# Moving operands of the weight matmuls in two, four or eight parts, at other addresses modulo 256

## The chip, the cores and the metric

One core of a Trainium2 chip runs the kernel. The time is device time in microseconds of one execution, as the median of several; lower is better. The kernel before takes 845.64 us, the median of 3 runs (844.99 to 845.87).

## What is computed

Two transformer blocks over 256 tokens of width 1024, in float32. What matters here is that nearly all the work is products of the activations with weight matrices, 139 MB of which are read once.

```python
def first_block(x, ...):
    h = rms_norm(x, norm_mix_pre[l])
    proj = h @ w_in[l]                       # attention, recurrence and gate columns
    ...
    merged = (gates[..., :D] * (o_sb @ w_sb_out[l]) + gates[..., D:] * (o_rw @ w_rw_out[l]))
    x = x + rms_norm(merged @ w_o[l], norm_mix_post[l])
    h = rms_norm(x, norm_ffn_pre[l])
    f = (jax.nn.silu(h @ w_ffn_gate[l]) * (h @ w_ffn_up[l])) @ w_ffn_down[l]
    x = x + rms_norm(f, norm_ffn_post[l])

def second_block(x, mem, ...):
    x = x + hybrid_mixer(rms_norm_2(x, g_mix), w_in, conv_w, g_attn_out, g_conv_out, w_out)
    x = x + memory_cross_attention(rms_norm_2(x, g_xattn), rms_norm_2(mem, g_mem), w_q_mem, w_kv_mem, w_o_mem)
    x = x + squared_relu_mlp(rms_norm_2(x, g_mlp), w_up, w_down)
    return rms_norm_2(x, g_final)
```

## The kernel before, in words

Activations lie feature by token: a tile `[128, chunks, 256]` holds 128 features of each chunk on the partitions and its 256 tokens along the row. Weights come in slabs of 128 x 1024 float32 (512 KB): `slab` (line 182) loads one into `wraw` from the SyncE queue (L192), ScalarE rounds it to float32r in `whi` (L193), VectorE takes the remainder into `wlo` (L194). Activations are split in the same way into a hi and a lo tile by `split` (L277, L278), or by `scaled` with a gain (L325, L326). A product is then three matmuls for each 128 rows: `whi` with hi, `whi` with lo, `wlo` with hi. `block` (line 240) issues them (L258): the weight block of 128 x 128 is the stationary operand, the activation chunk of 256 tokens the moving one, so a slab of 256 columns and 512 rows is 24 matmuls. With `tok` the sides are exchanged: the activations are stationary, 128 tokens at a time, and the weights move (256 columns). The last matrix, `w_down_2`, is done that way too with 512 moving columns (`tokens`, through `mm`, L273); `ah` and `al` are the stationary side there.

The tiles in question: `xh`, `xl` hold the normed input of most products; `gh`, `gl` that of the first recurrence columns; `zh`, `zl` half of the merged branches; `sh`, `sl`, `oh`, `ol` the two branch outputs; `memh`, `meml` the memory; `fh`, `fl` the gated hidden rows of the first block (22 chunks); `yh`, `yl` the mixer's and `xoh`, `xol` (names in the trace of `oh`, `ol` in `cross`) the cross attention's output; `ah`, `al` the hidden rows of the last block (32 chunks).

The order of the work is the order of the code: `plan` lists the slabs, `next_slab` keeps three ahead, and smaller steps of the recurrence and the attentions are woven in between slabs. Each engine runs its instructions in program order.

Addresses are set by the order of allocation and by `shift` (line 119), which allocates a spare tile of a given number of bytes. Before the change the weights `whi` and `wlo` begin at multiples of 256 bytes, all tiles named above except `ah` and `al` at 192 past one, and `ah`, `al` at 64 past one. A chunk's row is 1024 bytes, so each chunk of a tile begins at the same place modulo 256.

Of the kernel before, what the change touches and what calls it, by code (L numbers as in the profile page):

```python
# [17 lines left out]
P = 128  # L18
T = 256
# [71 lines left out]


class Net:
    def __init__(self, ctx, tc, io):
        self.tc, self.nc, self.io = tc, tc.nc, io
        self.last_table = None
        self.queue, self.ready = [], []
        self.t2 = 3
        self.side = None
        nc = self.nc  # L100
        pool = lambda name, bufs=1, **k: ctx.enter_context(tc.tile_pool(name=name, bufs=bufs, **k))
        self.keep = pool("keep")
        self.cst = self.keep.tile([P, NRES], F32, name="cst")
        self.vec = self.keep.tile([P, NVEC], F32, name="vec")
        self.small = self.keep.tile([P, 8], F32, name="small")
        self.ones = self.keep.tile([P, P], F32, name="ones")
        self.pr = pool("wraw", 3)
        self.ph = pool("whi", 4)
        self.pl = pool("wlo", 4)


        acts = pool("acts")
        self.shift(acts, PHASE)
        self.xh = acts.tile([P, KC, T], F32R, name="xh")
        self.xl = acts.tile([P, KC, T], F32R, name="xl")
        self.zh = acts.tile([P, NP, T], F32R, name="zh")
        self.zl = acts.tile([P, NP, T], F32R, name="zl")

# [123 lines left out]
    def block(self, ps, name, g, b, xh, xl, tok):  # L242
        per = blocks(name)
        hi, lo, k0, m = self.next_slab(name, g * per + b)
        if isinstance(xh, list):
            xh, xl = xh[b], xl[b]
        cols = width(name) // P
        for c in range(cols):
            cc = slice(c * P, (c + 1) * P)
            for k in range(m):  # L250
                for t, (w, a) in enumerate(((hi, xh), (hi, xl), (lo, xh))):
                    first = b == 0 and c == 0 and k == 0 and t == 0
                    last = b == per - 1 and c == cols - 1 and k == m - 1 and t == 2
                    if tok:
                        lhsT, rhs = a[:, k0 + k, cc], w[:, k, :]
                    else:
                        lhsT, rhs = w[:, k, cc], a[:, k0 + k, :]
                    self.nc.tensor.matmul(ps[:, c, :], lhsT, rhs, start=first, stop=last,  # L258
                                          skip_group_check=True)

# [14 lines left out]
    def split(self, src, hi, lo):  # L275

        self.nc.scalar.copy(hi, src)  # L277
        self.nc.vector.tensor_sub(lo, src, hi.bitcast(F32))  # L278
# [13 lines left out]

    def rstd_sum(self, pool, parts, width, tag, square=None):

        ps = self.ax("ssum")
        for i, p in enumerate(parts):
            self.mm(ps[:, :T], self.ones, p, start=i == 0)
        lg = pool.tile([P, T], F32, tag="t1", name="lg", bufs=1)
        r = pool.tile([P, T], F32, tag=tag, name=tag)
        self.act(lg, ps[:, :T], AF.Ln, bias=self.eps, scale=1.0 / width)  # L300
        self.act(r, lg, AF.Exp, scale=-0.5)
        if square is not None:
            self.act(square, lg, AF.Exp, scale=-1.0)
        return r
# [15 lines left out]
    def scaled(self, src, gname, hi, lo, first=0):  # L320

        for i, s in enumerate(src, first):
            for j in range(2):
                k, g = 2 * i + j, self.v(gname, 2 * i + j)
                self.nc.scalar.activation(hi[:, k, :], s[:, j, :], AF.Copy, scale=g)  # L325
                self.nc.vector.scalar_tensor_tensor(lo[:, k, :], s[:, j, :], g, hi[:, k, :].bitcast(F32),  # L326
                                                    op0=ALU.mult, op1=ALU.subtract)
# [16 lines left out]
    def normed(self, pool, src, r, gname, hi, lo):  # L344

        for i, s in enumerate(src):
            h = pool.tile([P, 2, T], F32, tag="t2", name="nh", bufs=self.t2)
            for j in range(2):
                self.nc.vector.scalar_tensor_tensor(
                    h[:, j, :], s[:, j, :], self.v(gname, 2 * i + j), r, op0=ALU.mult, op1=ALU.mult)  # L350
            self.split(h, hi[:, 2 * i:2 * i + 2, :], lo[:, 2 * i:2 * i + 2, :])

# [74 lines left out]
def first(n):  # L427
    nc, tc = n.nc, n.tc
    with ExitStack() as ctx:
# [4 lines left out]
        one = ctx.enter_context(tc.tile_pool(name="one", bufs=1))  # L434
        n.shift(one, 608)
        s4 = ctx.enter_context(tc.tile_pool(name="s4", bufs=14))
        dr = ctx.enter_context(tc.tile_pool(name="dr", bufs=1, space=DRAM))
        n.shift(ctx.enter_context(tc.tile_pool(name="gap", bufs=1)), 640)

# [14 lines left out]
        xg = start.enter_context(tc.tile_pool(name="xg", bufs=1))  # L454
        gh = xg.tile([P, KC, T], F32R, name="gh")
        gl = xg.tile([P, KC, T], F32R, name="gl")
        n.scaled(xp, "norm_mix_pre", gh, gl)
# [317 lines left out]
        nc.scalar.copy(idb, n.c("ident"))  # L775
        sh = b4.tile([P, NP, T], F32R, tag="b4", name="sh")
        sl = b4.tile([P, NP, T], F32R, tag="b4", name="sl")
        pz, zm = {}, {}
# [27 lines left out]
        def sb_values(j):  # L806
            wt = zm[j][1]
            po = n.sx("po")
            for t, o, wc in ((0, slice(0, T), slice(0, T)), (1, slice(P, T), slice(T, 384))):
                for r_, rr in enumerate(half):  # L810
                    i = 2 * j + r_
                    n.mm(po[rr, o], vs_[:, t, 64 * i:64 * i + 64], wt[:, r_, wc], start=t == 0)
            of = tmp.tile([P, T], F32, tag="c2", name="of", bufs=3)
            nc.vector.tensor_copy(of, po[:, :T])
            n.split(of, sh[:, j, :], sl[:, j, :])

# [153 lines left out]
        def normalized():  # L970
# [3 lines left out]
            nc.sync.dma_start(flat(gb), park[1])  # L974
            oh, ol = norm["o"] = [s4.tile([P, NP, T], F32R, tag="s4", name=k) for k in ("oh", "ol")]
            pv = {}
# [11 lines left out]
            for i in range(2):  # L988
# [9 lines left out]
                nc.vector.tensor_add(yi, yi, gb[:, ii, :])  # L998
                n.split(yi, oh[:, ii, :], ol[:, ii, :])
            yield  # L1000
# [13 lines left out]
        for g in range(4):  # L1014
# [5 lines left out]
            hi, lo = (n.zh, n.zl) if g < 2 else (n.xh, n.xl)  # L1020
            n.split(t, hi[:, 2 * g:2 * g + 2, :], lo[:, 2 * g:2 * g + 2, :])

# [29 lines left out]
def ffn(n, tmp, wide, filler):  # L1052
    nc, tc = n.nc, n.tc
    with tc.tile_pool(name="ffn", bufs=1, reuse_waits="tile") as pool:
# [4 lines left out]
        n.table("silu_and_others")  # L1059
        fh = pool.tile([P, FF // P, T], F32R, name="fh")  # L1060
        fl = pool.tile([P, FF // P, T], F32R, name="fl")
        for g in range(FF // 256):
# [7 lines left out]
            nc.vector.tensor_mul(m, m, s)  # L1070
            n.split(m, fh[:, 2 * g:2 * g + 2, :], fl[:, 2 * g:2 * g + 2, :])
        n.table("natural_log_exp_and_others")
# [3 lines left out]
def memory(n, mem, wide, tmp, kT, vm):  # L1076
# [3 lines left out]
    nc.scalar.dma_start(m.rearrange("p c t -> p (c t)"), n.io["mem"])  # L1080
    mh = mem.tile([P, KC, T], F32R, name="memh")
    ml = mem.tile([P, KC, T], F32R, name="meml")
    n.scaled(pairs(m), "g_mem_2", mh, ml)
    acc = n.squares(tmp, pairs(m))
    r = pair(n.rstd_sum(mem, [acc], D, "rk"))
    rt = n.rstd_tok(mem, [acc], D, out=n.small[:, 4:6])
# [17 lines left out]
def hybrid(n, tmp, kv):  # L1104
    nc, tc = n.nc, n.tc
    with ExitStack() as ctx:
        pool = ctx.enter_context(tc.tile_pool(name="hyb", bufs=1, reuse_waits="tile"))
        yh = pool.tile([P, KC, T], F32R, name="yh")
        yl = pool.tile([P, KC, T], F32R, name="yl")
        r2 = pool.tile([P, T], F32, name="r2")  # L1110
        rs = []

        def norms():
            acc = n.squares(tmp, pairs(n.x))
            rs.append(pair(n.rstd_sum(pool, [acc], D, "rm", r2)))
            rs.append(n.rstd_tok(pool, [acc], D))
# [89 lines left out]
        def conv_norm():  # L1206
            rc = n.rstd(tmp, pairs(cv), 512, "rs")
            kv(4, n.ax("kv").rearrange("p (c t) -> p c t", c=2))
            n.normed(tmp, pairs(cv), rc, "g_conv_out_2", yh[:, NP:, :], yl[:, NP:, :])

# [3 lines left out]
def cross(n, tmp, kT, vm, kv):  # L1214
    nc, tc = n.nc, n.tc
    with ExitStack() as ctx:
        pool = ctx.enter_context(tc.tile_pool(name="xat", bufs=1, reuse_waits="tile"))
        oh = pool.tile([P, KC, T], F32R, name="xoh")
        ol = pool.tile([P, KC, T], F32R, name="xol")
        n.scaled(pairs(n.x), "g_xattn_2", n.xh, n.xl)  # L1220
# [52 lines left out]
        def values(h):  # L1273
# [8 lines left out]
            hh = slice(2 * h, 2 * h + 2)  # L1282
            nc.scalar.copy(oh[:, hh, :], po)
            nc.vector.tensor_sub(ol[:, hh, :], po, oh[:, hh, :].bitcast(F32))

# [15 lines left out]
def mlp(n, tmp, out):  # L1301
    nc, tc = n.nc, n.tc
    with ExitStack() as ctx:
        pool = ctx.enter_context(tc.tile_pool(name="mlp", bufs=1, reuse_waits="tile"))
        n.shift(pool, 832 - PHASE)
        ah = pool.tile([P, 32, T], F32R, name="ah")
# [144 lines left out]
```

## Time and profile before

| what | value |
|---|---|
| median of 3 runs | 845.64 us |
| the profiled execution's own time | 845.12 us |
| its span | 843.4 us |
| TensorE busy | 97% of the span, 6508 matmul records |
| weight loads busy | 92% |
| VectorE, ScalarE busy | 67%, 55% |
| DMA | 142.88 MB, mean 169 GB/s |

The span runs from the first to the last instruction of the profiled execution; 1.7 us of its time lie outside. Busy time counts an instruction from start to end. Matmuls are pipelined: one starts long before the one ahead of it ends, so the mean duration of a matmul (some 280 ns) is not its price. The distance from one start to the next is, and the chain in order of time shows it as the time of a piece divided by its count. A matmul of float32 operands leaves two records, one of float32r operands a single one; both are shown as f32.

### The profile page before, as it was taken

How to read it: one execution, taken by the hardware profiler on the slowest of the kernel's cores; microseconds unless marked ns; L12 is line 12 of the kernel's file. 1: busy time of each engine (PE TensorE's matmuls, PEld its weight loads, DVE VectorE, ACT ScalarE, POOL GpSimd, SP SyncE). 2: the span in 40 equal slices, each digit the busy share in tenths (PEclk: the TensorE clock that was granted, in tenths of full speed). 3: DMA queues.
4: the chain of work that ended last, by engine and by line, in shares of the span. 5: the costliest groups of instructions: out<-in, count | busy, mean ns of one | idle time of the engine just before them, and what ended most of it. 6: DMA issues, size and time to landing. Idle time of an engine off the chain costs nothing.

```text
span 843.4 us, 15763 instructions
## 1 busy us (share of the span) xinstructions
PE 818.9 (97%) x6508; PEld 777.1 (92%) x6508; DVE 565.0 (67%) x790; ACT 464.5 (55%) x714; POOL 5.7 (1%) x18
## 2 busy tenths in 40 slices
PE   5999998999999999999999999999999999999996
PEld 5898987999999999999999998999999999988884
DVE  6958689455978776666544876689676676654543
ACT  6587355643577654445444656457455575553432
POOL 0001001000000000000000000000000000000000
PEclk9999999999999999999999999999999999999998
DMA  8444433543464755555566464455534555555551
GB/s 289 141 150 152 141 127 119 163 148 99 136 245 147 228 189 185 194 181 191 167 192 184 155 209 146 147 180 193 179 100 155 194 177 178 198 188 186 194 181 51
DMA packets 44632, 142.88 MB, mean 169 GB/s; under 512 B 8977, under 2 KB 9745, under 8 KB 44305
## 3 DMA queue, kind: packets, MB, share of 16 engines
q1 hardware_dynamic: 43840, 139.25, 50.9%
q10 hardware_dynamic: 720, 2.63, 0.8%
q8 instruction: 51, 0.84, 0.4%
q14 instruction: 21, 0.16, 0.1%
HBM read 139.17 MB, written 2.69 MB: 168 GB/s over the span
## 4 chain that ended last, share of the span: by engine, by line
PE 81%; DVE 9%; ACT 4%; DMA 3%; issue 2%; DVEq 0%; ACTq 0%; SPq 0%
PE mm L258 59%; PE mm L273 11%; DVE wlo L194 3%; PE pz L273 2%; ACT whi L193 1%; DMA mraw<-in_mem 1%; PE rw L258 1%; PE po L273 1%; PE px L273 1%; PE mgnh L273 1%; PE ssum L273 1%; PE nv L273 1%; DVE prw L747 1%; PE kv L258 1%; DVE xl L326 1%
## 5 line engine op out<-in xcount | busy, mean ns | idle before, releaser
L194 DVE TENSOR_TENSOR wlo<-wraw,whi 128x1024 fp32r<-128x1024 f32 x254 | 308.2, 1215 | 191.0 <-ACT whi L193 190.2
L193 ACT CAST whi<-wraw 128x1024 fp32r<-128x1024 f32 x254 | 264.6, 1044 | 282.8 <-PE mm L258 162.5
L258 PE MATMUL mm<-xh,whi 128*128 128x256 f32 x1120 | 316.5, 283 | 0.0
L258 PE MATMUL mm<-xh,wlo 128*128 128x256 f32 x1120 | 313.4, 280 | 1.9 <-DVE wlo L194 1.9
L258 PE MATMUL mm<-xl,whi 128*128 128x256 f32 x1120 | 313.4, 280 | 0.0
L258 PEld LDWEIGHTS mm<-xh,wlo 128*128 128x128 f32 x1120 | 212.1, 189 | 3.2 <-DVE wlo L194 2.9
L258 PEld LDWEIGHTS mm<-xh,whi 128*128 128x128 f32 x1120 | 210.9, 188 | 3.7 <-issue 2.1
L258 PEld LDWEIGHTS mm<-xl,whi 128*128 128x128 f32 x1120 | 210.7, 188 | 0.9 <-issue 0.6
L273 PE MATMUL mm<-wlo,ah 128*128 128x512 f32 x128 | 50.6, 395 | 0.0
L273 PE MATMUL mm<-whi,al 128*128 128x512 f32 x128 | 50.6, 395 | 0.0
L273 PE MATMUL mm<-whi,ah 128*128 128x512 f32 x128 | 50.6, 395 | 0.0
L258 PE MATMUL mm<-fh,whi 128*128 128x256 f32 x176 | 49.5, 281 | 0.0
L258 PE MATMUL mm<-fl,whi 128*128 128x256 f32 x176 | 49.5, 281 | 0.0
L258 PE MATMUL mm<-fh,wlo 128*128 128x256 f32 x176 | 49.5, 281 | 0.0
L258 PEld LDWEIGHTS mm<-fh,wlo 128*128 128x128 f32 x176 | 33.8, 192 | 0.0
L258 PEld LDWEIGHTS mm<-fh,whi 128*128 128x128 f32 x176 | 33.0, 188 | 0.0
L258 PEld LDWEIGHTS mm<-fl,whi 128*128 128x128 f32 x176 | 33.0, 188 | 0.0
L273 PEld LDWEIGHTS mm<-whi,al 128*128 128x128 f32 x128 | 24.1, 188 | 5.8
L273 PEld LDWEIGHTS mm<-wlo,ah 128*128 128x128 f32 x128 | 24.1, 188 | 5.8
L273 PEld LDWEIGHTS mm<-whi,ah 128*128 128x128 f32 x128 | 24.1, 188 | 5.7
L258 PE MATMUL rw<-gh,whi 128*128 128x256 f32 x48 | 14.9, 310 | 8.6 <-ACT whi L193 8.6
L258 PE MATMUL mm<-memh,whi 128*128 128x256 f32 x64 | 18.5, 288 | 0.0
(352 smaller groups left out, 1377.4 us busy)
## 6 DMA issues: line engine op xcount, KB each, us to landing
wraw<-in_w_up SPq DMA_DIRECT2D x32, 512.0 KB, 3.3
wraw<-in_w_down SPq DMA_DIRECT2D x32, 512.0 KB, 3.3
wraw<-in_w_in SPq DMA_DIRECT2D x24, 512.0 KB, 4.1
wraw<-in_w_ffn_gate SPq DMA_DIRECT2D x22, 512.0 KB, 3.4
wraw<-in_w_ffn_up SPq DMA_DIRECT2D x22, 512.0 KB, 3.3
wraw<-in_w_ffn_down SPq DMA_DIRECT2D x20, 512.0 KB, 3.6
wraw<-in_w_gate SPq DMA_DIRECT2D x16, 512.0 KB, 3.3
wraw<-in_w_kv_mem SPq DMA_DIRECT2D x16, 512.0 KB, 3.3
```

Of the source, the lines that this page charges most:

```text
L193: nc.scalar.copy(hi[:, :w], raw[:, :w])
L194: nc.vector.tensor_sub(lo[:, :w], raw[:, :w], hi[:, :w].bitcast(F32))
L258: self.nc.tensor.matmul(ps[:, c, :], lhsT, rhs, start=first, stop=last, skip_group_check=True)
L273: self.nc.tensor.matmul(out, lhsT, rhs, start=start, stop=stop, skip_group_check=True)
L326: self.nc.vector.scalar_tensor_tensor(lo[:, k, :], s[:, j, :], g, hi[:, k, :].bitcast(F32), op0=ALU.mult, op1=ALU.subtract)
L747: nc.vector.tensor_mul(pr, left[:, r:r + 4, :].rearrange("p r (o i) -> p r o i", o=1).to_broadcast([P, 4, 16, 16]), right.rearrange("p (o ...
```

## The change

A new helper `parted` makes the tile for a hi or a lo operand in `n` parts. Part h holds tokens h x 256/n to (h+1) x 256/n of all chunks, and the parts are laid out with a stride that is `jump` bytes modulo 256. A chunk as a moving operand is then n runs of 256/n tokens, and the starts of the runs go on by 64 or 128 bytes modulo 256 from one to the next. The values and the order of the tokens are the same. `in_parts` views a contiguous tile in the same shape, for the sources of the splits and for the output of the matmul.

By tile: `x` 2 parts with 128 bytes, `z`, `g` and `f` 4 with 128, `mem` 2 with 64, `y` 8 with 64, `xo` 4 with 64. `sh`, `sl`, `oh`, `ol` are only viewed in two parts, with no jump.

The padding and three spare tiles that go or change move other tiles: `sh`, `sl` then begin 224 and `oh`, `ol` 96 bytes past a multiple of 256, `ah`, `al` 192; `meml` begins at 64, and the other parted tiles at 192 as before. `rk` and `r2` and the tile `rm` go to other pools or tags, which makes room. No instruction is added, removed or moved on TensorE, VectorE, ScalarE or SyncE; the shapes of the operands change (256 becomes 2 x 128, 4 x 64 or 8 x 32). POOL has one `shift` memset less.

```diff
+def parted(pool, chunks, name, n, jump):
+    w = chunks * T // n
+    t = pool.tile([P, n, w + (jump // 4 - w) % 64], F32R, name=name)
+    return t[:, :, :w].rearrange("p h (k s) -> p k h s", s=T // n)
+
+def in_parts(t, n):
+    return t.rearrange("p (h s) -> p h s", h=n) if len(t.shape) == 2 else t.rearrange("p k (h s) -> p k h s", h=n)
...
-        self.xh = acts.tile([P, KC, T], F32R, name="xh")
-        self.xl = acts.tile([P, KC, T], F32R, name="xl")
-        self.zh = acts.tile([P, NP, T], F32R, name="zh")
-        self.zl = acts.tile([P, NP, T], F32R, name="zl")
+        self.xh, self.xl = (parted(acts, KC, k, 2, 128) for k in ("xh", "xl"))
+        self.zh, self.zl = (parted(acts, NP, k, 4, 128) for k in ("zh", "zl"))
...
                     if tok:
-                        lhsT, rhs = a[:, k0 + k, cc], w[:, k, :]
+                        o, lhsT, rhs = ps[:, c, :], a[:, k0 + k, c], w[:, k, :]
                     else:
-                        lhsT, rhs = w[:, k, cc], a[:, k0 + k, :]
-                    self.nc.tensor.matmul(ps[:, c, :], lhsT, rhs, start=first, stop=last,
-                                          skip_group_check=True)
+                        o, lhsT, rhs = in_parts(ps[:, c, :], a.shape[2]), w[:, k, cc], a[:, k0 + k]
+                    self.nc.tensor.matmul(o, lhsT, rhs, start=first, stop=last, skip_group_check=True)
...
     def split(self, src, hi, lo):
 
+        if len(hi.shape) > len(src.shape):
+            src = in_parts(src, hi.shape[2])
         self.nc.scalar.copy(hi, src)
         self.nc.vector.tensor_sub(lo, src, hi.bitcast(F32))
...
-                self.nc.scalar.activation(hi[:, k, :], s[:, j, :], AF.Copy, scale=g)
+                t = in_parts(s[:, j, :], hi.shape[2])
+                self.nc.scalar.activation(hi[:, k], t, AF.Copy, scale=g)
...
-        n.shift(one, 608)
...
-        n.shift(ctx.enter_context(tc.tile_pool(name="gap", bufs=1)), 640)
...
-        gh = xg.tile([P, KC, T], F32R, name="gh")
-        gl = xg.tile([P, KC, T], F32R, name="gl")
+        n.shift(xg, 224)
+        gh, gl = (parted(xg, KC, k, 4, 128) for k in ("gh", "gl"))
...
-        sh = b4.tile([P, NP, T], F32R, tag="b4", name="sh")
-        sl = b4.tile([P, NP, T], F32R, tag="b4", name="sl")
+        sh, sl = (in_parts(b4.tile([P, NP, T], F32R, tag="b4", name=k), 2) for k in ("sh", "sl"))
...
-        fh = pool.tile([P, FF // P, T], F32R, name="fh")
-        fl = pool.tile([P, FF // P, T], F32R, name="fl")
+        fh, fl = (parted(pool, FF // P, k, 4, 128) for k in ("fh", "fl"))
...
-    mh = mem.tile([P, KC, T], F32R, name="memh")
-    ml = mem.tile([P, KC, T], F32R, name="meml")
+    mh, ml = (parted(mem, KC, k, 2, 64) for k in ("memh", "meml"))
...
-    r = pair(n.rstd_sum(mem, [acc], D, "rk"))
+    rk = mem.tile([P, T], F32, name="rk")
+    r = pair(n.rstd_sum(tmp, [acc], D, None, out=rk))
...
-        yh = pool.tile([P, KC, T], F32R, name="yh")
-        yl = pool.tile([P, KC, T], F32R, name="yl")
-        r2 = pool.tile([P, T], F32, name="r2")
+        yh, yl = (parted(pool, KC, k, 8, 64) for k in ("yh", "yl"))
+        r2 = tmp.tile([P, T], F32, tag="rs", name="r2")
...
-            rs.append(pair(n.rstd_sum(pool, [acc], D, "rm", r2)))
+            rs.append(pair(n.rstd_sum(tmp, [acc], D, "ra", r2)))
...
-        oh = pool.tile([P, KC, T], F32R, name="xoh")
-        ol = pool.tile([P, KC, T], F32R, name="xol")
+        oh, ol = (parted(pool, KC, k, 4, 64) for k in ("xoh", "xol"))
...
-        n.shift(pool, 832 - PHASE)
+        n.shift(pool, 512)
         ah = pool.tile([P, 32, T], F32R, name="ah")
         al = pool.tile([P, 32, T], F32R, name="al")
```

Left out are the places where an index `[:, a:b, :]` becomes `[:, a:b]`, and the new argument `out` of `rstd_sum`.

## Rows read from the trace of the kernel before

**Rows 1.** The page, its first part: busy time of each engine.

```profile
PE 818.9 (97%) x6508; PEld 777.1 (92%) x6508; DVE 565.0 (67%) x790; ACT 464.5 (55%) x714; POOL 5.7 (1%) x18
```

**Rows 2.** The page, its fourth part: the chain's shares by line.

```profile
PE mm L258 59%; PE mm L273 11%; DVE wlo L194 3%; PE pz L273 2%; ACT whi L193 1%; DMA mraw<-in_mem 1%; PE rw L258 1%; PE po L273 1%; PE px L273 1%; PE mgnh L273 1%; PE ssum L273 1%; PE nv L273 1%; DVE prw L747 1%; PE kv L258 1%; DVE xl L326 1%
```

**Rows 3.** Windows: us, busy of each engine (instructions), granted clock, DMA share, GB/s.

```profile
289.00:402.00 113.00, 113.00 (x962) 113.00 (x961) 75.52 (x82) 57.11 (x66) 0.00 (x0) 1.00 0.58 189
...
695.00:745.00 50.00, 50.00 (x444) 50.00 (x443) 32.88 (x37) 28.82 (x38) 0.00 (x0) 1.00 0.58 192
747.00:834.00 87.00, 87.00 (x375) 70.09 (x374) 39.14 (x35) 31.84 (x35) 0.00 (x0) 1.00 0.49 162
```

**Rows 4.** The chain in order of time, its longest pieces: start us, us, what.

```profile
288.81 175.25 PE mm L258 x1488
...
694.44 51.70 PE mm L258 x456
746.14 88.21 PE mm L273 x378
```

**Rows 5.** Timeline of TensorE: start us, us, engine, line, operation, operands, count.

```profile
666.75 0.36 PE L273 MATMUL rtok<-ones,sqa 128*128 128x1 f32 x2
666.97 0.36 PE L258 MATMUL mm<-xh,whi 128*128 128x256 f32 x1
```

**Rows 6.** The chain in order of time, float32 matmuls of 128 and 512 columns.

```profile
160.41 1.79 PE px L273 x16
...
165.03 1.78 PE py L273 x16
...
210.48 1.72 PE mean L273 x4
```

**Rows 7.** The chain in order of time, shorter pieces of line 258.

```profile
97.25 7.39 PE mm L258 x61
...
154.56 5.85 PE mm L258 x48
...
162.20 2.83 PE mm L258 x24
...
271.39 16.99 PE mm L258 x142
...
489.68 11.41 PE mm L258 x96
...
539.29 5.85 PE mm L258 x48
545.57 22.61 PE mm L258 x192
568.62 5.65 PE kv L258 x48
...
620.93 2.72 PE mm L258 x24
...
641.33 25.44 PE mm L258 x216
```

**Rows 8.** Groups by shape, TensorE: busy us, mean ns | idle before.

```profile
L258 PE MATMUL mm<-xh,whi 128*128 128x256 f32 x1120 | 316.5, 283 | 0.0
...
L258 PE MATMUL mm<-fh,whi 128*128 128x256 f32 x176 | 49.5, 281 | 0.0
...
L258 PE MATMUL mm<-yh,whi 128*128 128x256 f32 x64 | 18.0, 281 | 0.0
...
L258 PE MATMUL rw<-gl,whi 128*128 128x256 f32 x48 | 14.7, 306 | 0.0
...
L258 PE MATMUL mm<-zh,whi 128*128 128x256 f32 x32 | 9.0, 281 | 0.0
```

**Rows 9.** Groups by shape, ScalarE: writes in one run and in pieces of 64.

```profile
L277 ACT CAST sh<-of 128x256 fp32r<-128x256 f32 x4 | 1.6, 407 | 8.9 <-DVE of L814 8.9
L604 ACT COPY KB<-kk 128x256 f32<-128x256 f32 x4 | 1.6, 424 | 0.0
```

More of the change, by code (lines that the diff above doesn't have):

```diff
@@ L291, in sumsq, with rstd_sum @@
         return a2
-    def rstd_sum(self, pool, parts, width, tag, square=None):
+    def rstd_sum(self, pool, parts, width, tag, square=None, out=None):
         ps = self.ax("ssum")
@@ L298, in rstd_sum @@
         lg = pool.tile([P, T], F32, tag="t1", name="lg", bufs=1)
-        r = pool.tile([P, T], F32, tag=tag, name=tag)
+        r = pool.tile([P, T], F32, tag=tag, name=tag) if out is None else out
         self.act(lg, ps[:, :T], AF.Ln, bias=self.eps, scale=1.0 / width)
@@ L324, in scaled @@
                 k, g = 2 * i + j, self.v(gname, 2 * i + j)
-                self.nc.scalar.activation(hi[:, k, :], s[:, j, :], AF.Copy, scale=g)
-                self.nc.vector.scalar_tensor_tensor(lo[:, k, :], s[:, j, :], g, hi[:, k, :].bitcast(F32),
+                t = in_parts(s[:, j, :], hi.shape[2])
+                self.nc.scalar.activation(hi[:, k], t, AF.Copy, scale=g)
+                self.nc.vector.scalar_tensor_tensor(lo[:, k], t, g, hi[:, k].bitcast(F32),
                                                     op0=ALU.mult, op1=ALU.subtract)
@@ L350, in normed @@
                     h[:, j, :], s[:, j, :], self.v(gname, 2 * i + j), r, op0=ALU.mult, op1=ALU.mult)
-            self.split(h, hi[:, 2 * i:2 * i + 2, :], lo[:, 2 * i:2 * i + 2, :])
+            self.split(h, hi[:, 2 * i:2 * i + 2], lo[:, 2 * i:2 * i + 2])
 def staggered(count, *stages, apart=1):
@@ L814, in sb_values @@
             nc.vector.tensor_copy(of, po[:, :T])
-            n.split(of, sh[:, j, :], sl[:, j, :])
+            n.split(of, sh[:, j], sl[:, j])
         early.close()
@@ L974, in normalized @@
             nc.sync.dma_start(flat(gb), park[1])
-            oh, ol = norm["o"] = [s4.tile([P, NP, T], F32R, tag="s4", name=k) for k in ("oh", "ol")]
+            oh, ol = norm["o"] = [in_parts(s4.tile([P, NP, T], F32R, tag="s4", name=k), 2) for k in ("oh", "ol")]
             pv = {}
@@ L998, in normalized @@
                 nc.vector.tensor_add(yi, yi, gb[:, ii, :])
-                n.split(yi, oh[:, ii, :], ol[:, ii, :])
+                n.split(yi, oh[:, ii], ol[:, ii])
             yield
@@ L1020, in first @@
             hi, lo = (n.zh, n.zl) if g < 2 else (n.xh, n.xl)
-            n.split(t, hi[:, 2 * g:2 * g + 2, :], lo[:, 2 * g:2 * g + 2, :])
+            n.split(t, hi[:, 2 * g:2 * g + 2], lo[:, 2 * g:2 * g + 2])
 def branch_add(n, tmp, pool, w, hi, lo, gname, filler, after, side=False):
@@ L1070, in ffn @@
             nc.vector.tensor_mul(m, m, s)
-            n.split(m, fh[:, 2 * g:2 * g + 2, :], fl[:, 2 * g:2 * g + 2, :])
+            n.split(m, fh[:, 2 * g:2 * g + 2], fl[:, 2 * g:2 * g + 2])
         n.table("natural_log_exp_and_others")
@@ L1208, in conv_norm @@
             kv(4, n.ax("kv").rearrange("p (c t) -> p c t", c=2))
-            n.normed(tmp, pairs(cv), rc, "g_conv_out_2", yh[:, NP:, :], yl[:, NP:, :])
+            n.normed(tmp, pairs(cv), rc, "g_conv_out_2", yh[:, NP:], yl[:, NP:])
         plain_add(n, "w_out_2", yh, yl, conv_norm)
@@ L1282, in values @@
             hh = slice(2 * h, 2 * h + 2)
-            nc.scalar.copy(oh[:, hh, :], po)
-            nc.vector.tensor_sub(ol[:, hh, :], po, oh[:, hh, :].bitcast(F32))
+            n.split(po, oh[:, hh], ol[:, hh])
         def attention():
```

## The prediction

> **What bounds the kernel now.** I read the page first for the engines' shares, then the chain of waits, then the long stretches as windows, then the same chain in order of time, which gives the pace of a matmul, and last the groups by shape for the counts.
>
> TensorE is busy 97% of the 843.4 us span [rows 1]. In the chain that ended last, the matmuls of lines 258 and 273 that write `mm`, the weight matmuls, hold 70% of the span [rows 2]. In the long stretches nothing else is close: from 289 to 402 us TensorE is busy all of the time, at a granted clock of 1.00, the level of 2.4 GHz, and VectorE 75.5 of 113 us, ScalarE 57.1, the DMA engines 58% [rows 3]. So a matmul that starts earlier there ends the kernel earlier.
>
> What matters is the pace, not the busy time, since busy spans of matmuls overlap. The chain in order of time gives it: 1,488 matmuls in 175.25 us, 117.8 ns each, and later 456 in 51.70 us, 113.4 ns each [rows 4]. Both stretches are line 258, 256 columns, three terms per 128 rows, the second with the same tile `xh` at the same address as the first half of the former. So the shape alone doesn't set the pace. Other pieces of the chain stand at one of these two levels as well: 192 in 22.61 us, 117.8, and 216 in 25.44, 117.8 [rows 7]. TensorE is busy throughout and waits for no engine there, so the reading of the operands is the suspect: each matmul reads its moving rows while the next weights load.
>
> Three rows bound how far the pace can fall. A matmul of a single column (`rtok`) is still followed 0.11 us later (two of them start at 666.75, the next matmul at 666.97) [rows 5]. Matmuls of 128 float32 columns take 1.79/16 = 112 ns whether their moving operand is two parts of 64 with a jump between them (`px`, 256 bytes, a multiple of 256) or one run (`py`, 1.78). And 512 float32 columns (`mean`) take 1.72/4 = 430 ns a record, 0.84 ns a column, while 512 columns of the down projection take 88.21/378 = 233.4 ns [rows 4, 6]: those operands are float32r, which goes at about twice the rate (0.44 ns a column at 113.4). By estimate from the two, 512 columns at twice the rate of `mean` would take 215 ns if nothing held them, so 18 ns are lost there; and no matmul of 256 columns is seen under about 112 ns.
>
> **The change part by part.** No instruction is added, removed or moved on TensorE, VectorE, ScalarE or SyncE; POOL loses one one-column memset at the start, which nothing waits for. What changes is where operands lie.
>
> 1. *The moving operands in parts.* Seven pairs of tiles (x, f, mem, xo, y, g, z) are read in two, four or eight parts whose starts differ by 64 or 128 bytes modulo 256. The weights keep their place at a multiple of 256, so a matmul that before ran at one fixed distance from the weights now changes it one, three or seven times. That is 3 x (1120 + 176 + 64 + 64 + 64 + 48 + 32) = 4,704 matmuls [rows 8] (mem, xo and y have 64 each, and the three terms are alike). I take it that no lasting slow level can then form, and that the quicker of the two levels seen, 113.4, holds throughout. The parted matmuls that stand in the chain at the slow level: 1,488 [rows 4]; then 96 + 48 + 2 x 192 + 216, and 94 of the 142 at 271 us (48 of those are the `kv(5)` with weights as moving operand, which keep theirs); before 222 us 61 + 2 x 48 + 3 x 24 [rows 7] (where a piece is counted two or three times, one row stands for those like it). That is 2,326 + 229 = 2,555, times 117.8 - 113.4 = 4.4 ns: **11.2 us**. The other 4,704 - 2,555 - 456 = 1,693 lie in short pieces at either level, partly behind casts and DMAs: 0 to 7.4 us, of which I take 1.2, near the lower end, as the waits of other engines there stay.
>
> 2. *The down projection.* Its `ah` and `al`, the stationary side there, move from 64 to 192 bytes past a multiple of 256, while the moving weights stay. The distance changes sign only. The 256-column matmuls of `kv` with weights as moving operand stand at that other distance before, and show the same two levels: 48 in 5.65 us, 117.7, and 24 in 2.72 us, 113.3 [rows 7]. So I take 0. The ends: 18.4 ns less on 378 matmuls, 7.0 us gained [rows 4, 6]; one step of 4.4 ns for each 256 columns more, 3.3 us lost.
>
> 3. *`sh`, `sl`, `oh`, `ol`* are viewed in two parts without a jump, and lie at 224 and 96 bytes instead of 192: 192 matmuls, by one step either way 0.8 us; taken as 0.
>
> 4. *The writers.* ScalarE and VectorE now write hi and lo in pieces. Where ScalarE writes pieces of 64 already (`KB`, 424 ns for 128x256) it takes 17 ns more than in one run (`sh`, 407) [rows 9]. Work of these two hides under TensorE in the long stretches; where they are on the chain at the start of a stage it is a few operations each: 0 taken, 0.4 us the bound.
>
> 5. *`r2`, `rk` and the `rm` tile* change pools or tags. Their new buffers are used again only after groups whose readers ended several slabs earlier, so no wait ends later for it: 0.
>
> Sum: 11.2 + 1.2 = 12.4 us. The profiled execution took 845.12 us (845.64 is the median of the runs, 0.5 more): 845.1 - 12.4 = **832.7 us**.
>
> **The rivals.**
>
> *It goes further (0.28).* The parts could remove the rest of the loss too. Then the pace ends at the load of the weights, about 111.9 ns: 2,555 x 5.9 ns = 15.1, 456 x 1.5 = 0.7, and 1.7 of the short pieces: 827.6 us; and with the down projection at its bound 820.6. For it: `rtok` and `px` show that pace [rows 5, 6]. Against it: no matmul of 256 columns does, and `px` moves at half the rate. The Trainium skill (TensorE: Matmul & The Clock Gate, Back-to-back issue gap) states N/2.4 + 2.5 ns for an isolated matmul, which is 109.2 ns for 256 columns and 215.8 for 512; the down projection's 233.4 is not that, and by it, as an estimate, the whole could come near 813.
>
> *Nothing changes (0.10).* If the two levels come from how a stretch is entered and not from addresses, a parted operand is entered as before and each stretch falls to one level or the other again: 845.1, give or take the short pieces. For it: both levels stand at equal addresses. Against it: the 18 ns lost at 512 columns are the mean over all of the 378, and the float32 matmuls of 512 columns set the pace that they miss [rows 4, 6]; something costs time within the matmul. The Trainium skill (TensorE: Matmul & The Clock Gate, Step-by-step: what each phase is for) says that TensorE has two independent SBUF read ports, so that loading the next weights takes nothing from the running matmul; by that rule the change would be worth nothing, and these rows speak against it.
>
> *Slower (0.20).* Each jump could break the stream of reads. The trace has no such matmul at the quicker rate: `px` has a jump at half the rate, under a weight load that hides it. There are 3,552 matmuls with one jump, 960 with three and 192 with seven, 7,776 jumps; from 1.6 ns a jump on (12.4 us / 7,776) the forecast gain is gone. If the levels stay and each of 4,704 matmuls loses a quarter of a step, 1.1 ns, 85% of it on the chain, that is 849.5 us; with a whole step of 4.4 ns, 862.7.
>
> **How the numbers follow.** The forecast has 0.42, the rivals 0.28, 0.10 and 0.20. About 0.2%, 1.7 us, is what a measurement of this kernel can tell from no change. Faster is forecast and first rival, 0.70; same 0.10; slower 0.20. The range runs from 816 (the first rival's 820.6 less the short pieces that I left out) to 849, just under the near end of the slower rival; what lies beyond is mostly that rival's dearer half.
>
> **What would show it.** Right: the piece of 1,488 matmuls that now begins at 288.8 us takes about 168.7 us, 113.4 ns each; the pieces of 96, 192 and 216 take 10.9, 21.8 and 24.5 us; `fl`, `xl` and the rest of VectorE and ScalarE keep their mean durations within some per cent; the 378 of the down projection stay near 88 us. Wrong: the first piece still at 117.8 (second rival), or above (third), or at 112 and below (first); or a shorter piece followed by a wait for `wlo` or `wraw` that was not there, since a slab must now be ready every 24 x 113.4 ns = 2.72 us instead of 2.83.

## The result, and the profile after

The changed kernel takes 852.23 us (median of 4 runs, 849.85 to 853.31), the kernel before 845.32 in the same comparison (4 runs, 844.06 to 845.87). The ratio is 1.0083, with a 95% interval of 1.0065 to 1.0100: **slower by 6.9 us**, where 832.7 was forecast and the range ended at 849. The execution that was profiled took 849.85 us, the quickest of the four, with a span of 848.2 against 843.4; so the two traces account for 4.8 of the 6.9 us.

The shares of the engines hardly moved. The page's first and fourth parts of the changed kernel:

```profile
PE 827.0 (98%) x6508; PEld 787.7 (93%) x6508; DVE 565.4 (67%) x790; ACT 466.0 (55%) x714; POOL 5.6 (1%) x17
...
PE 89%; DVE 7%; ACT 2%; DMA 1%; issue 1%; SPq 0%; ACTq 0%; DVEq 0%
PE mm L268 66%; PE mm L282 11%; DVE wlo L204 2%; PE pz L282 2%; DMA wraw<-in_w_rw 1%; PE rw L268 1%; PE po L282 1%; PE px L282 1%; PE mgnh L282 1%; PE nv L282 1%; PE ssum L282 1%; DVE prw L757 1%; PE kv L268 1%; ACT whi L203 1%; DVE pr L739 1%
```

The line that was L258 is L268 now, and L273 is L282. They hold 77% of the span in the chain, where they held 70% [rows 2], and the other engines' parts shrank. The chain's shares by engine in the kernel before were:

```profile
PE 81%; DVE 9%; ACT 4%; DMA 3%; issue 2%; DVEq 0%; ACTq 0%; SPq 0%
```

Matmuls that go slower take up waits that were there anyway, so not all of their loss reaches the end: TensorE is busy 8.1 us more than before (827.0 against 818.9 [rows 1]) and idle 3.3 us less, and the span grows by the 4.8 that are left. TensorE's own waits for other engines show nothing new. The waits view (line waiting, who ended it, us in total, times, longest), of the kernel before and then of the changed kernel:

```profile
PE rw L258 <- ACT whi L193: 8.6, 1, 8.6
PE pz L273 <- DVE zm L795: 3.1, 2, 2.9
PE mm L258 <- DVE wlo L194: 2.5, 3, 1.3
```

```profile
PE rw L268 <- ACT whi L203: 8.9, 1, 8.9
PE pz L282 <- DVE zm L804: 3.1, 2, 2.7
PE mm L268 <- DVE wlo L204: 0.8, 3, 0.4
```

The pace tells the story. The chain of the changed kernel in order of time (start us, us, what):

```profile
288.55 176.73 PE mm L268 x1488
...
490.82 11.45 PE mm L268 x96
...
547.01 23.16 PE mm L268 x192
...
576.30 23.17 PE mm L268 x192
...
670.58 11.44 PE mm L268 x96
...
698.83 53.86 PE mm L268 x456
752.69 86.55 PE mm L282 x378
```

The piece of 1,488 (x, then f) went from 117.8 to 118.8 ns a matmul, the 456 from 113.4 to 118.1 [rows 4], the pieces of 192 from 117.8 to 120.6 [rows 7]. Of these pieces only the down projection went the other way, from 233.4 to 229.0. Windows isolate `f`, which is the only moving operand from 402 to 464 us. The same window, in the kernel before and then in the changed one (us, busy of each engine with its instructions, granted clock, DMA share, GB/s):

```profile
402.00:464.00 62.00, 62.00 (x528) 62.00 (x528) 29.86 (x30) 27.59 (x35) 0.00 (x0) 1.00 0.61 182
```

```profile
402.00:464.00 62.00, 62.00 (x519) 62.00 (x518) 29.55 (x29) 26.95 (x34) 0.00 (x0) 1.00 0.61 179
```

In 62 us 519 matmuls fit where 528 did, at the same granted clock. For every tile the distance from one start to the next can be averaged over the trace (for 256 columns distances over 130 ns, where something else stood between, are left out; the count is of all matmuls). "Quick" is the share of distances under 116 ns, and "stationary" marks the products in which the tile is the stationary side and the weights move:

| tile (matmuls) | parts, jump | before, ns (quick) | after, ns (quick) | difference x count |
|---|---|---|---|---|
| x (3,360) | 2, 128 | 116.1 (0.39) | 118.1 (0.00) | +6.7 us |
| f (528) | 4, 128 | 117.8 (0) | 120.0 (0) | +1.2 |
| y (192) | 8, 64 | 117.8 (0) | 123.2 (0) | +1.0 |
| mem (192) | 2, 64 | 113.8 (0.89) | 118.0 (0.02) | +0.8 |
| xo (192) | 4, 64 | 116.7 (0.24) | 118.7 (0.07) | +0.4 |
| g, z (240) | 4, 128 | 117.5 (0.09) | 120.0 (0) | +0.6 |
| s, o (192) | 2, no jump, start 224 and 96 | 114.1 (0.84) | 119.1 (0.11) | +1.0 |
| x stationary (192) | | 117.8 (0) | 114.4 (0.78) | -0.7 |
| mem stationary (192) | | 115.5 (0.52) | 118.0 (0.22) | +0.5 |
| down projection (383 of 512 columns) | | 233.3 | 228.9 | -1.7 |

That is 9.8 us of TensorE by this count, of which 4.8 reach the end of the profiled execution. In the kernel before, the pace of x is a mix of two levels, 113.4 and 117.8; in the changed kernel the quick one is gone.

### The profile page after: what moved, and what is told of

It is laid out like the page before. It is cut to its first block, busy times and chain, and to the rows that moved or that the text cites. A ratio compares the mean times of both kernels' runs of the same rounds, so it can differ in the third digit from the quotient of the medians.

```text
span 848.2 us, 15766 instructions
## 1 busy us (share of the span) xinstructions
PE 827.0 (98%) x6508; PEld 787.7 (93%) x6508; DVE 565.4 (67%) x790; ACT 466.0 (55%) x714; POOL 5.6 (1%) x17
## 4 chain that ended last, share of the span: by engine, by line
PE 89%; DVE 7%; ACT 2%; DMA 1%; issue 1%; SPq 0%; ACTq 0%; DVEq 0%
PE mm L268 66%; PE mm L282 11%; DVE wlo L204 2%; PE pz L282 2%; DMA wraw<-in_w_rw 1%; PE rw L268 1%; PE po L282 1%; PE px L282 1%; PE mgnh L282 1%; PE nv L282 1%; PE ssum L282 1%; DVE prw L757 1%; PE kv L268 1%; ACT whi L203 1%; DVE pr L739 1%
## 5 line engine op out<-in xcount | busy, mean ns | idle before, releaser
L268 PE MATMUL mm<-xh,whi 128*128 128x256 f32 x1120 | 317.8, 284 | 0.0
L268 PE MATMUL mm<-xh,wlo 128*128 128x256 f32 x1120 | 314.6, 281 | 0.6 <-DVE wlo L204 0.6
L268 PE MATMUL mm<-xl,whi 128*128 128x256 f32 x1120 | 314.7, 281 | 0.0
L268 PEld LDWEIGHTS mm<-xh,whi 128*128 128x128 f32 x1120 | 210.5, 188 | 3.7 <-issue 2.8
L268 PEld LDWEIGHTS mm<-xh,wlo 128*128 128x128 f32 x1120 | 210.5, 188 | 1.7 <-DVE wlo L204 1.3
L268 PEld LDWEIGHTS mm<-xl,whi 128*128 128x128 f32 x1120 | 210.6, 188 | 0.9 <-issue 0.7
L282 PE MATMUL mm<-whi,al 128*128 128x512 f32 x128 | 50.4, 394 | 0.0
L282 PE MATMUL mm<-wlo,ah 128*128 128x512 f32 x128 | 50.2, 392 | 0.0
L268 PE MATMUL mm<-fh,wlo 128*128 128x256 f32 x176 | 49.7, 283 | 0.0
L268 PE MATMUL mm<-fl,whi 128*128 128x256 f32 x176 | 49.7, 283 | 0.0
L268 PE MATMUL mm<-fh,whi 128*128 128x256 f32 x176 | 49.7, 283 | 0.0
L282 PE MATMUL mm<-whi,ah 128*128 128x512 f32 x128 | 49.7, 388 | 0.0
L268 PEld LDWEIGHTS mm<-fh,whi 128*128 128x128 f32 x176 | 33.1, 188 | 0.0
L268 PEld LDWEIGHTS mm<-fh,wlo 128*128 128x128 f32 x176 | 33.1, 188 | 0.0
L268 PEld LDWEIGHTS mm<-fl,whi 128*128 128x128 f32 x176 | 33.1, 188 | 0.0
L282 PEld LDWEIGHTS mm<-wlo,ah 128*128 128x128 f32 x128 | 24.0, 188 | 5.6
L282 PEld LDWEIGHTS mm<-whi,ah 128*128 128x128 f32 x128 | 24.0, 188 | 5.3
L282 PEld LDWEIGHTS mm<-whi,al 128*128 128x128 f32 x128 | 24.1, 188 | 4.8
L268 PE MATMUL rw<-gh,whi 128*128 128x256 f32 x48 | 14.8, 308 | 8.9 <-ACT whi L203 8.9
L268 PE MATMUL mm<-memh,whi 128*128 128x256 f32 x64 | 18.8, 293 | 0.0
```

What stands on the lines that cost most here:

```text
L268: self.nc.tensor.matmul(o, lhsT, rhs, start=first, stop=last, skip_group_check=True)
L282: self.nc.tensor.matmul(out, lhsT, rhs, start=start, stop=stop, skip_group_check=True)
```

## The experiments

Theories at the start: **A**, a jump in the moving operand costs by itself, and more jumps cost more (the slower rival; 118.1, 120.0 and 123.2 ns for two, four and eight parts suggest it). **B**, the place of the moving bytes against those of the weights, modulo 256, sets the pace.

### The same parts, with no shift between them

```diff
-        self.xh, self.xl = (parted(acts, KC, k, 2, 128) for k in ("xh", "xl"))
+        self.xh, self.xl = (parted(acts, KC, k, 2, 0) for k in ("xh", "xl"))
...
-        yh, yl = (parted(pool, KC, k, 8, 64) for k in ("yh", "yl"))
+        yh, yl = (parted(pool, KC, k, 8, 128) for k in ("yh", "yl"))
```

and likewise 0 for z, g, f, mem and xo.

> The changed kernel with the same number of parts, but with part starts that do not move modulo 256 (the eight parts of y go on by 128 bytes, as an unparted row would). Theory A, a jump itself costs: the pace stays as in the changed kernel, about 118.1 ns for x, 120.0 for f, 122.5 for y, and the time stays near 852. Theory B, the place of the moving bytes against the weights' modulo 256 sets the pace: the two levels of 113.4 and 117.8 come back in x, f and y, and the time comes back to 843 to 848.

Measured: 842.63 us against 843.78, ratio 0.9983 [0.9971, 0.9995]. The chain in order of time, and the window of `f`:

```profile
288.48 175.25 PE mm L268 x1488
...
573.45 22.10 PE mm L268 x192
...
693.65 51.71 PE mm L268 x456
745.36 86.53 PE mm L282 x378
```

```profile
402.00:464.00 62.00, 62.00 (x528) 61.95 (x527) 29.86 (x30) 27.59 (x35) 0.00 (x0) 1.00 0.60 185
```

The times of the first and third piece are those of the kernel before to 0.01 us [rows 4], with the changed kernel's number of parts, its instructions and real jumps between the parts (768 to 5,376 bytes from the end of one to the start of the next). A jump that is neutral modulo 256 costs nothing; theory A falls. This kernel and the changed one differ in nothing but the shifts modulo 256, so the shifts are what the time was lost to. The 1.1 us gained are near the 1.7 of the down projection, which kept its new place, less 0.9 for `s` and `o`, which kept theirs.

### The parts of the change, at three other starts

```diff
-PHASE = 192
+PHASE = 64
```

and the same with 128; for 0 the spare tile is left out.

> The changed kernel with PHASE 64 for 192: all parted tiles begin at 64 bytes past a multiple of 256, the weights stay at 0. Theory A: the paces don't move (118.1, 120.0, 122.5), time near 852. Theory B: the paces move, most of all for f (four parts of 128) and y (eight of 64), whose distance to the weights' reading would be held nearly constant; some start must then lie under 113.4. For x with two parts of 128, starts of 192 and 64 hold the same two places in exchanged order, so x moves least.

> The changed kernel with PHASE 128: parted tiles begin at 128 past a multiple of 256. Theory A: 118.1, 120.0, 122.5 again. Theory B: other paces, with f and y apart from x, and one of the starts 0, 64, 128 clearly quicker than 192 for y.

> The changed kernel with no spare tile ahead of the activations: parted tiles begin at a multiple of 256, like the weights. Theory A: 118.1, 120.0, 122.5 again. Theory B: other paces; with start and weights at one place I expect the slowest of the four starts for y, above 122.5.

One execution each: 852.34, 853.31 and 847.93 us, against 843.78 for the kernel before. Pace in ns by start of the tile, in bytes past a multiple of 256:

| start | x (2, 128) | f (4, 128) | y (8, 64) | down projection: ah, al at that start |
|---|---|---|---|---|
| 192 (the change) | 118.1 | 120.0 | 123.2 | 228.9 |
| 64 | 118.0 | 120.0 | 122.2 | 233.3 |
| 128 | 118.6 | 120.0 | 120.6 | 233.3 |
| 0 | 117.8 | 117.3 | 120.6 | 226.7 |

The window of `f` with start 0:

```profile
402.00:464.00 62.00, 62.00 (x531) 62.00 (x530) 29.59 (x29) 27.81 (x34) 0.00 (x0) 1.00 0.60 181
```

The paces move with the start, which A excludes, but not in the way that B had expected. x moves little, as it had said, by 0.1 ns between 192 and 64. f, which was to move most along with y, stands at 120.0 at three starts and moves only at 0. y goes from 123.2 to 120.6; its 122.2 at start 64 shows no move, since y stands at 122.2 at start 192 as well in the run below that puts x back. B had expected some start under 113.4 and 0 as the slowest for y: no start lies under 113.4 for f or y, and for y 0 and 128 are the quickest. So B was right that the place matters and wrong as to which place is good. The last column was not sought: the stationary side has its places too, and 0 is the best of the four.

### Other jumps

```diff
-        fh, fl = (parted(pool, FF // P, k, 4, 128) for k in ("fh", "fl"))
+        fh, fl = (parted(pool, FF // P, k, 4, 192) for k in ("fh", "fl"))
```

with x 2 and 64, z 4 and 64, g 4 and 192, mem 2 and 128, y 8 and 192, xo 4 and 128.

> The changed kernel with other jumps at the same numbers of parts: x 2 parts with 64 (start of xl then 64), z 4 with 64, g and f 4 with 192, mem 2 with 128, y 8 with 192, xo 4 with 128. Theory B (the distance to the weights' bytes, not the jump as such): paces of f, y and xo move to other values than 120.0, 123.2 and 118.7; xo with 4 parts of 128 goes to 120.0 as f had it. Theory C, that any jump which is not a multiple of 256 costs alike: f stays at 120.0, y near 123, xo 118.7. If a jump gives under 113.4 anywhere, there is something to gain from the idea; I give that one chance in four.

Measured in one execution: 847.0 us, against 844.77 for the kernel before. The window of `f`:

```profile
402.00:464.00 62.00, 62.00 (x532) 61.95 (x531) 30.24 (x31) 28.26 (x36) 0.00 (x0) 1.00 0.61 187
```

f stands at 116.7 ns, y at 120.0, xo at 120.0, where f had stood with the same four parts of 128. So the jump and its direction matter: at start 192, four parts that go on by 128 give 120.0 in f, z, g and xo alike, four that go on by 192 (64 back) 116.7 in f and 116.8 in g, four that go on by 64 118.7 in xo (the change) and z (this run). At this start 192 is the only shift that was clearly quicker than the slow level; at others f with 128 (117.3 at start 0) and xo with 64 (116.8 at start 128) came under 117.8 too. Under 113.4 there is nothing. Theory C, that every shift costs alike, falls.

### x alone put back

```diff
-        self.xh, self.xl = (parted(acts, KC, k, 2, 128) for k in ("xh", "xl"))
+        self.xh, self.xl = (parted(acts, KC, k, 2, 0) for k in ("xh", "xl"))
```

> The changed kernel with x alone at part starts that do not move modulo 256. x is 3,360 of the 4,704 parted matmuls; it went from a mean of 116.1 to 118.1 ns, so 3,360 x 2.0 = 6.7 us should come back less what waits hide, and 0.6 us of the products with x as the stationary side go: near 846 to 847. If the loss sat in the smaller tiles instead, the time stays at 850 or above.

Measured: 845.73 us, ratio to the kernel before 1.0009 [0.9994, 1.0024]. The chain:

```profile
288.24 176.43 PE mm L268 x1488
...
696.27 51.70 PE mm L268 x456
747.97 86.53 PE mm L282 x378
```

x comes back to a mean of 116.1 ns and 0.38 quick, and about 6 of the 6.9 us with it: against the kernel before (844.77 here) 1.0 us is left, which can't be told from nothing. The other tiles' losses less the down projection's gain are still 3.6 us of TensorE by the count of the table above; most of that doesn't reach the end.

### One number in the kernel before

```diff
-        n.shift(pool, 832 - PHASE)
+        n.shift(pool, 768 - PHASE)
```

> The kernel before with one number changed: ah and al begin at a multiple of 256 (spare tile of 576 for 640 bytes). Theory B: the 383 matmuls of 512 columns go from 233.3 to 226.7 ns as in the run with start 0, 2.5 us less, near 842.0 against 844.5. If the quicker pace there came from the parts of the other tiles, it stays at 233.3 and the time doesn't move.

Measured: **841.13 us** against 844.77, ratio 0.9961 [0.9948, 0.9974]: quicker than both kernels. The chain:

```profile
286.73 175.25 PE mm L258 x1488
...
692.27 51.70 PE mm L258 x456
743.97 85.71 PE mm L273 x378
```

The 378 take 226.7 ns each, 2.5 us less than before [rows 4], as expected. The other 1.1 of the 3.6 us is not shown to come from the edit: in this execution other tiles stood at the quick level more often (x 0.45 of its distances, against 0.39). This trace also shows what addresses do not decide. In the window of `z`, from 235 to 245 us, line 258 alone, first the kernel before and then this one (us, TensorE busy, matmuls, granted clock, DMA share, GB/s):

```profile
235.00:245.00 10.00, 10.00 (x87) 1.00 0.88 356
```

```profile
235.00:245.00 10.00, 10.00 (x91) 1.00 0.88 353
```

The code and every address are the same there, and yet `z` moves at 117.6 ns in one and 113.5 in the other.

### No parts, at the three other starts

The last kernel, with `PHASE` 64, 128 and 0 (for 0 the spare tile ahead of the activations is left out) and `ah`, `al` kept at 0:

```diff
-PHASE = 192
+PHASE = 64
```

> The kernel before, no operand parted, ah and al at 0 as in the last run, and all moving tiles beginning 64 bytes past a multiple of 256 in place of 192. Theory B: an unparted row has one distance to the weights, so each start has its own levels; the pair 113.4 and 117.8 belongs to 192. From the tiles s and o of the earlier runs, which lay unparted at 32, 96, 160 and 224 (116.8, 119.9, 117.9, 118.3 ns), I expect 115 to 120 here. The products with x as the stationary side go to about 113.5 ns, 0.8 us less. Were the two levels a matter of entry alone (theory D), they would be 113.4 and 117.8 at every start.

> The same with all moving tiles at 128 past a multiple of 256. Theory B: other paces than at 192 and 64, between 113 and 120. Theory D: 113.4 and 117.8 again.

> The same with all moving tiles at a multiple of 256, the place of the weights. Theory B: other paces than at 192; if the four parts of f at start 0 (117.3) are a sign, about 117. Theory D: 113.4 and 117.8 again. If any of the three starts holds 113.4 in the stretch of 1,488 matmuls, that version beats both kernels by some 6 us.

One execution each: 845.29, 851.02 and 856.23 us, against 844.95 for the kernel before. The chain's longest piece, the `kv` piece (weights move, `mem` is stationary) and the 456, for 64, 128 and 0:

```profile
288.74 175.25 PE mm L258 x1488
...
568.73 5.46 PE kv L258 x48
...
695.07 53.71 PE mm L258 x456
```

```profile
289.92 176.57 PE mm L258 x1488
...
572.02 5.69 PE kv L258 x48
...
700.38 54.11 PE mm L258 x456
```

```profile
290.92 178.54 PE mm L258 x1488
...
575.87 5.75 PE kv L258 x48
...
705.04 54.72 PE mm L258 x456
```

At 64 both levels are there, 113.4 and 117.8, and this execution fell to the quick one less often (x 0.09 of its distances, against 0.45). At 128 the stretch stands at 118.7 (a fifth of the distances lie under 116, but spread all through it), at 0 at 120.0, with no quick level in any long piece. So theory D, that the levels come from how a stretch is entered, holds between 192 and 64 and falls for 128 and 0. Two expectations missed: start 0 was to be near 117 and is the slowest, and at 64 the products with x as the stationary side were to go to 113.5 and went to 116.8, a mix of both levels.

The `kv` rows bear on the word "against" in theory B, since no run moved the weights. There the weights are the moving row and begin at 0 in every run, and only the stationary row is shifted: 113.8 ns at 64, 118.5 at 128, 119.8 at 0 (and 117.7 at 192 before [rows 7]), near the levels that the same starts of the moving row give. So for 256 columns the pace goes with the distance between the two rows, not with the place of the moving row alone. The pace of 120.0 that four parts of 128 have at 192, 64 and 128 is that of an unparted row that begins where the weights begin; that the cause is the same is not shown.

## Why the prediction was wrong

**The step that failed** is the first part of the sum: "I take it that no lasting slow level can then form, and that the quicker of the two levels seen, 113.4, holds throughout." The first half was half right: the pair of levels went away. But the level that was left is the slow one, 118.0 to 118.1 for two parts, and worse for four and eight. Stretches at 113.4 were seen only where the moving row runs on without a shift, at 64 or 192 from the stationary row modulo 256, and there only in some stretches. No row stood behind the choice of the quicker level. The prediction took the parts as something that breaks a bad relation; they break the good one as surely. The 11.2 us it expected from 2,555 slow matmuls became nothing, and the quick ones, 0.39 of x and 0.89 of mem, became slow. The row that could have warned was the 456 at 113.4 [rows 4]: what it stood to lose was priced at a rival's edge only.

**The slower rival** had the side right (0.20, and 852.23 lies between its ends of 849.5 and 862.7), but not the mechanism: it let each jump cost, and jumps cost nothing where they are multiples of 256. What it called a quarter of a step on every matmul was a whole step on the quick ones and half a step on f.

**The rival that nothing changes** had a premise that held, both levels at equal addresses, but addresses count as well. Beside it the prediction named a rule of the Trainium skill (TensorE: Matmul & The Clock Gate, Step-by-step: what each phase is for), two independent read ports, so that loading weights takes nothing from a running matmul. By that rule alone the place of the two rows should not matter, and these runs don't agree: with instructions and clock alike, 256 columns take 113.4 to 123.2 ns by address, and 512 columns 226.7 to 233.3. Whether the two reads are what meets, no run shows.

**What held.** The bound that the prediction drew from `rtok` and `px`: no tile of 256 columns averages under 113 ns in any run. The down projection inside its ends: taken as 0, measured 1.7 us gained. The writers: `xl` takes 482 ns a piece against 478, `fl` 684 against 685, and no wait was added. The groups moved to other pools cost nothing that the waits show.

**What was undersized.** `s`, `o`: 0.8 us either way, measured 1.0 lost. Their start did it more likely than their view in parts, since parts without a shift cost nothing elsewhere, and at 32, 96, 160 and 224 they lay between 116.7 and 119.9 in every run; the two were not tried apart.

**Still open:** what decides, at equal addresses, whether a stretch of unparted rows falls to 113.4 or 117.8, and what in the chip joins the two readings. A stretch mostly keeps its level, the 1,488 for 175 us, and the level differed between kernels whose code there was equal. Those ran on different chips, which is not excluded as a cause there, but one execution shows both levels too, with `xh` at one address [rows 4]. More was not tried, nor were four parts with 192 for all tiles. The runs at other starts and with other jumps are one execution each, so differences of about 1 ns between them decide nothing.

## What to carry to other kernels

When a stretch shows two paces for one instruction, find which of them the change could destroy before counting what it could win: a change that takes away the slow pace can take away the quick one too. Here the pace of matmuls whose weights change each time depended on where moving and stationary rows begin modulo 256; one spare tile of another size was worth 2.5 us (88.21 less 85.71 in the chain), and the parts lost 6.9. Price the pace from starts in the chain, by tile, and let one run try another place for each tile: each tile's pace is a result of its own.

## What the runs showed that was not expected

- A moving row in parts was free here: two, four and eight parts with jumps that are neutral modulo 256 gave the paces of one run.
- 256 columns, unparted rows against weights at 0, by start: 113.4 or 117.8 at 64 and 192; 118.7 at 128; 120.0 at 0, the slowest.
- With 512 moving columns at 0 the stationary rows' start sets the pace: 226.7 ns at 0, the quickest, 228.9 at 192, 233.3 at 64 and 128.
- Eight parts of 64 were the slowest operand of all, 123.2 ns, and 122.2 in another run at the same start and with the same shift.
